# Inverse square roots by one GpSimd power and one Newton step, and an instruction order searched anew

## The chip, the cores and the metric

The kernel runs on one core of a Trainium2 chip. The metric is the time of one execution in device microseconds (us); the profiler's span, from the first to the last instruction of the program, is a little shorter. The engines are called TensorE (PE in the rows; PEld is its weight load), VectorE (DVE), ScalarE (ACT), GpSimd (POOL) and SyncE (SP, which issues the loads).

## What is computed

Two blocks of a network for 512 positions and a width of 1024, all in float32. The first block normalises its input, projects it once, and runs two branches side by side: a recurrence over the positions (a state of 64 x 64 for each of 8 heads) and an attention over the 128 best keys of each query. The second block has two convolutions, an attention to a memory of 256 rows, three gates and a gated feed-forward layer. What matters here is that inverse square roots stand between the stages:

```python
def rmsnorm(x, g):
    xf = x.astype(jnp.float32)
    y = xf * lax.rsqrt(jnp.mean(xf * xf, axis=-1, keepdims=True) + NORM_EPS)
    return (y * g.astype(jnp.float32)).astype(x.dtype)
...
    kk = kk / jnp.maximum(jnp.sqrt(jnp.sum(kk * kk, axis=-1, keepdims=True)), 1e-12)
...
    y = rwkv7_scan(r, decay, k, v, kk, a)
    mu = jnp.mean(y, axis=-1, keepdims=True)
    var = jnp.mean(jnp.square(y - mu), axis=-1, keepdims=True)
    y = (y - mu) * lax.rsqrt(var + GN_EPS) * gn_g.astype(f32) + gn_b.astype(f32)
...
    _, idx = lax.top_k(score, topk)
```

## The kernel before

Activations lie with the width on the 128 partitions and the 512 positions along the free axis, in 76 buffers of 128x512 (`a`). A weight tile of 1024 rows by 128 columns (`wr`, 128x1024 in SBUF, four buffers) is loaded by SyncE, rounded by ScalarE into `wh`, and the rest is put into `wl` by VectorE (line 354). TensorE then forms a product of 128x512 out of 24 matmuls (eight times `wh` by the rounded activation, `wh` by its rest, `wl` by the rounded activation) in one of eight PSUM buffers (`ps`). Nearly every instruction passes through one helper, so its line is 341; lines 345 to 361 are helpers that may choose between two engines.

The work before the second block is called the **first part** here. It has these strands:

- the projections of the first block (24 weight tiles: k, r, v, latent, gates);
- the decay, the pair matrices of eight chunks of 64 positions, their inverse (31 dependent pairs of a product and an addition on VectorE, then small matmuls), and the **chain**: eight chunks, each needing the state of the one before;
- a group norm after each second chunk (four, `gn0` to `gn3`);
- the index scores, and for three blocks of queries sixteen rounds of a maximum of eight and a replacement on VectorE (`topk1` to `topk3`, tiles of 256, 384 and 512 columns);
- the attention heads (`att0` to `att3`);
- the memory: its norm, its keys (`memk0` to `memk7`: eight float32 products of 128x256 each, 16 records in the trace), and its values in two halves (`memv0`, `memv1`: 48 matmuls of 128x512 each; here the weights are the moving side, so the rows read `ps<-wh,a` and `ps<-wl,a`);
- the splits `y0` to `y7` of the two branches' results into a rounded half and a rest, on which the first matmuls of the output projection (`out0` to `out7`, first half; then the second half and all of the second block) wait.

The second block follows: long rows of dense matmuls, with 31-tap convolutions on VectorE beside them.

The order on every engine is made ahead of time by a planner in the file (class `Program`). It gives every operation a duration from a cost table, keeps a clock for each engine, and always takes the operation that can start first; where several can, the one of lowest rank. A rank is an operation's place in the source plus a level of its group, from the table `LEVEL`. So a change of the table moves operations on all engines, and the engines then run their lists strictly in order.

An inverse root, `rsqrt`, is called 15 times: nine times in the first part (the input's norm, the key norm of the recurrence, the index keys, the index queries, the memory, four group norms), twice between the blocks, once in the convolution's layer norm, once before the feed-forward layer, and once for each half of the output. Each call works on a tile `s` of 2 to 32 columns: one tensor_scalar that scales and adds epsilon, two integer instructions for a first guess, and three Newton steps of three instructions each, all on VectorE, each depending on the one before.

Of the kernel before, what the change touches and what calls it, by code (L numbers as in the profile page):

```python
# [8 lines left out]
F32 = mybir.dt.float32  # L9
F32R = mybir.dt.float32r  # L10
AF = mybir.ActivationFunctionType
ALU = mybir.AluOpType
# [13 lines left out]
NA = 76  # L26
NS = 12
LEVEL = {
# [12 lines left out]
}  # L41
MEMC = 4
BOOST = 0
# [43 lines left out]
class Program:  # L87
# [73 lines left out]
    def cost(self, who, op, outs, ins):  # L161
        n = outs[0].free_size()
# [9 lines left out]
        n = max(x.free_size() for x in outs + ins)  # L172
# [10 lines left out]
            return 0.069 + 0.064 * (scalar or narrow > 0 and op == "tensor_scalar") + n / (1920.0 if fast else 960.0)  # L183
        if who == "S":
            return (0.058 if ins[0].space == PSUM else 0.085) + 0.092 * (narrow + len(outs) - 1) + n / 1175.0
        return 0.07 + n / (1250.0 if op == "memset" else 440.0)

    def order(self):
        nodes = self.nodes
# [129 lines left out]
def build(tc, I, O, plan=None):  # L319
# [69 lines left out]
    def here():  # L389
        return len(prog.nodes) - 1  # L390

    V, S, G, PE, SY = (Queue(e, w) for e, w in ((nc.vector, "V"), (nc.scalar, "S"), (nc.gpsimd, "G"),
                                                 (nc.tensor, "PE"), (nc.sync, "SY")))
# [13 lines left out]
    cst = es.enter_context(tc.tile_pool(name="cst", bufs=1))  # L407
# [42 lines left out]
    for k in range(8):  # L450
        t = A()
# [30 lines left out]
    G.memset(hsum, 0.0)  # L482
    G.memset(hsum[0:64, 0:1], 1.0)
    G.memset(hsum[64:128, 1:2], 1.0)
    hav = cst.tile([128, 1], F32, name="hav")
    G.memset(hav, 1.0 / 64)
    chmask = A((128, 8, 64))
# [25 lines left out]
    def ts(eng, out, in0, s1, s2, op0, op1=None):  # L513
        if op1 is None:
            eng.tensor_scalar(out, in0, s1, None, op0=op0)
        else:
            eng.tensor_scalar(out, in0, s1, s2, op0=op0, op1=op1)
# [8 lines left out]
    ts(G, DP("hbg", 24), P_("b_gate", 0, 24), 0.5, None, ALU.mult)  # L526
    ts(G, DP("hln", 16), P_("ln_g", 0, 16), 0.5, None, ALU.mult)

    I32 = mybir.dt.int32

    def rsqrt(src, n, eps, op=ALU.add, scale=1.0):

        x, y, t = SM(n), SM(n), SM(n)
        ts(V, x, src, scale, eps, ALU.mult, op)
        ts(V, t.bitcast(I32), x.bitcast(I32), 1, None, ALU.logical_shift_right)
        ts(V, y.bitcast(I32), t.bitcast(I32), -1.0, float(0x5F3759DF), ALU.mult, ALU.add)
        for _ in range(3):
            V.tensor_mul(t, y, y)
            V.scalar_tensor_tensor(t, t, -0.5, x, op0=ALU.mult, op1=ALU.mult)
            V.scalar_tensor_tensor(y, t, 1.5, y, op0=ALU.add, op1=ALU.mult)  # L540
        return y


# [155 lines left out]
    for j in range(2):  # L699
        t = A()  # L700
# [638 lines left out]
    r2 = SM(4)  # L1339
# [358 lines left out]
```

## Time and profile before

| | us |
|---|---|
| median of three runs (1376.52 to 1382.12) | 1377.17 |
| the profiled execution: its time | 1377.95 |
| the profiled execution: its span | 1376.2 |
| TensorE busy | 1348.1 |
| VectorE busy | 1049.8 |
| ScalarE busy | 585.4 |
| GpSimd busy | 29.9 |

Busy time is the union of an engine's instructions. A matmul counts as busy while it waits in the pipeline, so a busy TensorE may still do little useful work; how dense it is can be read from how fast one matmul of 128x512 starts after another.

### The profile page before, as it was taken

The numbers are of one execution on the slowest core, as the hardware profiler recorded it, in microseconds if no ns is written. First come the engines' busy times: TensorE is split into PE (matmuls) and PEld (weight loads), VectorE is DVE, ScalarE is ACT, GpSimd is POOL, SyncE is SP. The second block draws the span as 40 slices with busy tenths as digits, with TensorE's granted clock in tenths as the row PEclk, the third lists the DMA queues.
The fourth block names the chain that finished last, engine by engine and source line by source line (L and its number), as shares of the span: only waits on it lengthen the run. The fifth ranks groups of instructions, "written<-read, shape, count | busy, mean of one in ns | idle before, by whom it ended". The sixth has DMA issues, their size and how long they took to land.

```text
span 1376.2 us, 18233 instructions
## 1 busy us (share of the span) xinstructions
PE 1348.1 (98%) x7032; PEld 1121.8 (82%) x7032; DVE 1049.8 (76%) x1902; ACT 585.4 (43%) x945; POOL 29.9 (2%) x68
## 2 busy tenths in 40 slices
PE   7999999999999999999999999999999999999997
PEld 6878877888888888888888878888888888888886
DVE  7699879999699999999993584444577788784333
ACT  6683455668353334322222372223444444442221
POOL 2010002100000000000000000000000000000000
PEclk9999988999999999999999999999999999999999
DMA  6203220031446221233333223233222333322321
GB/s 225 71 20 104 84 72 32 32 100 55 145 146 214 92 77 62 77 101 99 92 98 101 77 92 107 92 98 101 92 92 95 104 92 96 103 88 96 100 70 61
DMA packets 41927, 129.29 MB, mean 94 GB/s; under 512 B 4912, under 2 KB 7088, under 8 KB 41840
## 3 DMA queue, kind: packets, MB, share of 16 engines
q1 hardware_dynamic: 41840, 128.13, 28.8%
q8 instruction: 55, 0.90, 0.3%
q14 instruction: 32, 0.26, 0.1%
HBM read 123.91 MB, written 4.19 MB: 93 GB/s over the span
## 4 chain that ended last, share of the span: by engine, by line
PE 88%; DVE 7%; ACT 3%; issue 1%; POOL 0%; DMA 0%; DVEq 0%; POOLq 0%; ACTq 0%
PE ps L341 88%; DVE a L341 5%; ACT a L341 2%; DVE s L341 1%; DVE wl L354 0%; DVE a L354 0%; ACT a L346 0%; ACT wh L341 0%; DMA wr<-in_w_v 0%; POOL a L341 0%; DVE a L345 0%; POOL mm L341 0%; DVE x L345 0%; ACT a L350 0%; POOL gsel L341 0%
## 5 line engine op out<-in xcount | busy, mean ns | idle before, releaser
L341 PE MATMUL ps<-a,wh 128*128 128x512 f32 (+1 forms) x3276 | 1006.2, 388 | 0.2 <-ACT wh L341 0.2
L341 PEld LDWEIGHTS ps<-a,wh 128*128 128x128 f32 x3276 | 612.1, 188 | 123.5 <-ACT wh L341 0.8
L341 PE MATMUL ps<-a,wl 128*128 128x512 f32 (+1 forms) x1638 | 634.7, 388 | 0.5 <-DVE wl L354 0.5
L341 ACT ACTIVATE wh<-wr 128x1024 fp32r<-128x1024 f32 (+3 forms) x223 | 224.8, 1010 | 490.6 <-PE ps L341 362.3
L341 PEld LDWEIGHTS ps<-a,wl 128*128 128x128 f32 x1638 | 308.2, 188 | 62.8 <-DVE wl L354 1.0
L354 DVE TENSOR_TENSOR wl<-wr,wh 128x1024 fp32r<-128x1024 f32 (+3 forms) x223 | 257.9, 1159 | 78.2 <-ACT wh L341 76.8
L341 DVE SCALAR_TENSOR_TENSOR a<-a,par 128x511 f32<-128x511 f32 (+24 forms) x393 | 273.4, 730 | 5.5 <-ACT a L341 3.1
L341 DVE TENSOR_TENSOR a<-ps,a 128x512 f32<-128x512 f32 (+1 forms) x186 | 117.2, 632 | 113.2 <-PE ps L341 107.2
L341 ACT ACTIVATE a<-a 128x512 f32<-128x512 f32 (+5 forms) x184 | 112.3, 623 | 169.5 <-DVE a L341 151.2
L341 PE MATMUL ps<-a 128*64 128x64 f32 (+10 forms) x1060 | 134.3, 296 | 14.5 <-POOL a L341 7.5
L341 PEld LDWEIGHTS ps<-a 128*64 128x64 f32 (+5 forms) x1040 | 103.5, 170 | 27.3 <-DVE a L341 5.7
L341 DVE SCALAR_TENSOR_TENSOR a<-a 128x512 f32<-128x512 f32 (+3 forms) x112 | 67.7, 611 | 20.3 <-ACT a L341 19.4
L341 DVE TENSOR_TENSOR a<-a 128x512 f32<-128x512 f32 (+5 forms) x134 | 76.0, 585 | 3.0 <-ACT a L341 1.9
L341 ACT ACTIVATE a<-a,par 128x512 f32<-128x512 f32 (+1 forms) x89 | 65.1, 737 | 19.7 <-DVE a L341 18.0
L354 DVE TENSOR_TENSOR a<-a 128x512 fp32r<-128x512 f32 x72 | 48.4, 686 | 18.1 <-ACT a L341 16.1
L341 ACT ACTIVATE a<-ps 128x512 fp32r<-128x512 f32 (+5 forms) x77 | 42.1, 569 | 44.4 <-PE ps L341 33.5
L341 DVE SCALAR_TENSOR_TENSOR a<-a,ps 128x512 f32<-128x512 f32 x24 | 16.5, 686 | 55.5 <-PE ps L341 55.4
L341 ACT ACTIVATE a<-a,dpar 128x512 f32<-128x512 f32 (+2 forms) x57 | 41.6, 733 | 7.6 <-DVE a L341 7.3
L346 ACT ACTIVATE a<-ps 64x256 f32<-64x256 f32 (+5 forms) x74 | 29.5, 409 | 28.3 <-PE ps L341 26.9
L341 PE MATMUL ps<-ident,a 128*128 128x128 f32 x204 | 32.7, 286 | 1.0 <-ACT a L350 0.6
L341 PEld LDWEIGHTS ps<-ident,a 128*128 128x128 f32 x204 | 25.8, 155 | 7.2 <-ACT a L350 1.7
L341 PE MATMUL ps<-a,wr 128*128 128x256 f32 x128 | 29.6, 379 | 0.0
(113 smaller groups left out, 567.7 us busy)
## 6 DMA issues: line engine op xcount, KB each, us to landing
wr<-in_w_in SPq DMA_DIRECT2D x96, 512.0 KB, 3.6
wr<-in_w_up SPq DMA_DIRECT2D x44, 512.0 KB, 3.4
wr<-in_w_down SPq DMA_DIRECT2D x16, 512.0 KB, 3.5
a<-in_xt SPq DMA_DIRECT2D x16, 256.0 KB, 3.5
wr<-in_w_k SPq DMA_DIRECT2D x8, 512.0 KB, 3.6
wr<-in_w_v SPq DMA_DIRECT2D x8, 512.0 KB, 3.6
wr<-in_w_out SPq DMA_DIRECT2D x16, 256.0 KB, 2.7
wr<-in_w_att SPq DMA_DIRECT2D x8, 512.0 KB, 3.5
```

Source lines behind the costliest of these rows:

```text
L341: prog.add({self.who: (op, lambda: f(*a, **k))}, outs, ins)
L346: "S": ("activation", lambda: nc.scalar.activation(out, src, AF.Copy))}, [out], [src])
L354: prog.add({"V": ("tensor_sub", lambda: nc.vector.tensor_sub(out, x, y))}, [out], [x, y])
```

## The change

`rsqrt` keeps its first instruction, takes the power -0.5 of the result on GpSimd (a tensor_tensor against a constant tile `mhalf` of 128x32, filled once at the start), and makes one Newton step on VectorE. That is four VectorE instructions for twelve, and a handover to GpSimd and back. The planner's cost of a tensor_tensor on GpSimd rises by 0.5 us (the products of the chain are called tensor_mul there and keep theirs), and all 76 levels have new values.

```diff
 LEVEL = {
-    "att0": -0.214, "att1": 1.055, "att2": -0.113, "att3": 1.636, "base": 2.048, "chain": -0.643, "first":
+    "att0": -0.233, "att1": 0.828, "att2": 3.274, "att3": -0.202, "base": -0.147, "chain": -0.334, "first":
...
-    "memk4": 1.634, "memk5": 1.165, "memk6": -1.209, "memk7": 3.877, "memv0": -0.227, "memv1": -0.052, "norm":
+    "memk4": 3.276, "memk5": -0.212, "memk6": -1.07, "memk7": 3.939, "memv0": 3.63, "memv1": -0.234, "norm":
...
-        return 0.07 + n / (1250.0 if op == "memset" else 440.0)
+        return 0.07 + 0.5 * (op == "tensor_tensor") + n / (1250.0 if op == "memset" else 440.0)
...
+    mhalf = cst.tile([128, 32], F32, name="mhalf")
+    G.memset(mhalf, -0.5)
...
     def rsqrt(src, n, eps, op=ALU.add, scale=1.0):
 
         x, y, t = SM(n), SM(n), SM(n)
         ts(V, x, src, scale, eps, ALU.mult, op)
-        ts(V, t.bitcast(I32), x.bitcast(I32), 1, None, ALU.logical_shift_right)
-        ts(V, y.bitcast(I32), t.bitcast(I32), -1.0, float(0x5F3759DF), ALU.mult, ALU.add)
-        for _ in range(3):
-            V.tensor_mul(t, y, y)
-            V.scalar_tensor_tensor(t, t, -0.5, x, op0=ALU.mult, op1=ALU.mult)
-            V.scalar_tensor_tensor(y, t, 1.5, y, op0=ALU.add, op1=ALU.mult)
+        G.tensor_tensor(y, x, mhalf[:, 0:n], op=ALU.pow)
+        V.tensor_mul(t, y, y)
+        V.scalar_tensor_tensor(t, t, -0.5, x, op0=ALU.mult, op1=ALU.mult)
+        V.scalar_tensor_tensor(y, t, 1.5, y, op0=ALU.add, op1=ALU.mult)
         return y
```

Three places show what this does to the order. The first is VectorE at the root of the index queries (8 columns); `wr` and `x` with two sizes are the inverse's products and additions. Before:

```order
L341 TENSOR_SCALAR s<-ps 128x8
L341 TENSOR_TENSOR wr<-wr,a 128x23x9
L341 TENSOR_SCALAR s<-s 128x8
L341 TENSOR_TENSOR a<-wr,x_367 128x192
L341 TENSOR_SCALAR s<-s 128x8
L341 TENSOR_TENSOR wr<-wr,a 128x24x8
L341 TENSOR_TENSOR s<-s 128x8
L341 TENSOR_TENSOR a<-wr,x_367 128x175
L341 SCALAR_TENSOR_TENSOR s<-s 128x8
```

After, the same root is complete in:

```order
L341 TENSOR_SCALAR s<-ps 128x8
L341 SCALAR_TENSOR_TENSOR a<-a 128x512 x2
L341 TENSOR_TENSOR s<-s 128x8
L341 TENSOR_TENSOR a<-ps,a 128x512
L341 SCALAR_TENSOR_TENSOR s<-s 128x8
L354 TENSOR_TENSOR wl<-wr,wh 128x1024
L341 SCALAR_TENSOR_TENSOR s<-s 128x8
```

The root no longer stands between the steps of the inverse, and two gate products of 128x512 stand between its first instruction and the one that needs GpSimd's result.

The second is TensorE at the first half of the memory's values, `memv0`. Before, it begins in the middle of the attention:

```order
L341 MATMUL ps<-a 128x384 x2
L341 MATMUL ps<-a,wr 128x256 x8
L341 MATMUL ps<-a 128x128 x2
L341 MATMUL ps<-wh,a 128x512
L341 MATMUL ps<-ident,a 128x128
L341 MATMUL ps<-wl,a 128x512
L341 MATMUL ps<-wh,a 128x512 x2
```

After, it begins where the first half of the output projection (rows `a,wh` and `a,wl`) ends:

```order
L341 MATMUL ps<-a,wl 128x512
L341 MATMUL ps<-a,wh 128x512 x2
L341 MATMUL ps<-a,wl 128x512
L341 MATMUL ps<-wh,a 128x512
L341 MATMUL ps<-wl,a 128x512
L341 MATMUL ps<-wh,a 128x512 x2
```

All 48 matmuls of `memv0` have moved from the first part to behind it; the last memory key, `memk7`, has gone the other way.

The third is VectorE at the memory's norm, of which only the order after is shown (before, the four squares stand on ScalarE, line 360):

```order
L341 MATCH_REPLACE a<-s,a 128x512
L341 SCALAR_TENSOR_TENSOR a<-a,wi 128x384
L341 MAX s<-a 128x8
L361 TENSOR_TENSOR a<-a 128x512 x3
L341 TENSOR_TENSOR a<-a 128x512
```

Three of the four squares of the memory now stand on VectorE.

## Rows read from the trace of the kernel before

**Rows 1.** The page's busy times: engine, busy us (share of span), instructions.

```profile
PE 1348.1 (98%) x7032; PEld 1121.8 (82%) x7032; DVE 1049.8 (76%) x1902; ACT 585.4 (43%) x945; POOL 29.9 (2%) x68
```

**Rows 2.** Busy time by stretch; the columns stand in the first line.

```profile
core 0: us, PE busy (x) PEld busy (x) DVE busy (x) ACT busy (x) POOL busy (x), PEclk, DMA share, GB/s
0.00:65.00 65.00, 57.18 (x281) 46.43 (x282) 46.20 (x91) 42.22 (x69) 8.18 (x36) 1.00 0.48 157
...
140.00:195.00 55.00, 53.88 (x385) 44.88 (x384) 40.15 (x88) 25.77 (x40) 1.90 (x2) 0.94 0.26 82
195.00:275.00 80.00, 73.52 (x818) 63.09 (x818) 75.93 (x237) 49.18 (x117) 11.55 (x21) 0.91 0.11 38
275.00:352.50 77.50, 76.70 (x503) 64.98 (x502) 76.94 (x260) 55.95 (x135) 0.00 (x0) 1.00 0.25 79
352.50:1364.00 1011.50, 1010.75 (x4622) 841.63 (x4623) 731.85 (x1071) 365.50 (x484) 1.44 (x2) 1.00 0.31 99
```

**Rows 3.** TensorE's timeline at the first part's end: start, duration, engine, operation.

```profile
348.78 3.71 PE L341 MATMUL ps<-a 128*64 128x128 f32 x64
352.42 0.73 PE L341 MATMUL ps<-a,wh 128*128 128x512 f32 x2
...
374.34 3.61 PE L341 MATMUL ps<-a,wr 128*128 128x256 f32 x16
```

**Rows 4.** TensorE's timeline inside `memv0`.

```profile
285.54 0.62 PE L341 MATMUL ps<-wh,a 128*128 128x512 f32 x2
285.99 0.39 PE L341 MATMUL ps<-wl,a 128*128 128x512 f32 x1
286.22 0.62 PE L341 MATMUL ps<-wh,a 128*128 128x512 f32 x2
```

**Rows 5.** VectorE's timeline: the splits `y0` to `y2`, then `y3` behind one of `memk5`.

```profile
349.32 1.89 DVE L354 TENSOR_TENSOR a<-a 128x512 fp32r<-128x512 f32 x3
...
351.93 1.29 DVE L354 TENSOR_TENSOR a<-a 128x512 fp32r<-128x512 f32 x2
```

**Rows 6.** Timeline of the last root, which stands alone, and of TensorE behind it.

```profile
1366.04 0.16 DVE L341 TENSOR_SCALAR s<-ps 128x2 f32<-128x2 f32 x1 [1.37 <-PE ps L341]
1366.23 0.37 DVE L341 TENSOR_SCALAR s<-s 128x2 int32<-128x2 int32 x2
...
1368.01 0.36 DVE L341 SCALAR_TENSOR_TENSOR s<-s 128x2 f32<-128x2 f32 x2
...
1368.42 0.71 PE L341 MATMUL ps<-ident,s 128*128 128x128 f32 x4 [1.52 <-DVE s L341]
```

**Rows 7.** VectorE's timeline where the index root stands between the inverse's steps.

```profile
147.34 0.38 DVE L341 TENSOR_TENSOR wr<-wr,a 128x207 f32<-128x207 f32 x1
147.63 0.17 DVE L341 TENSOR_SCALAR s<-s 128x8 int32<-128x8 int32 x1
147.75 0.53 DVE L341 TENSOR_TENSOR a<-wr,x 128x192 f32<-128x192 f32 x1
```

**Rows 8.** VectorE's groups by shape: line, operation, count | busy us, mean ns.

```profile
L354 DVE TENSOR_TENSOR wl<-wr,wh 128x1024 fp32r<-128x1024 f32 x195 | 237.8, 1221 | 70.4 <-ACT wh L341 68.9
...
L341 DVE SCALAR_TENSOR_TENSOR a<-a 128x512 f32<-128x512 f32 x72 | 49.6, 689 | 20.3 <-ACT a L341 19.4
```

**Rows 9.** The one square that VectorE makes: count, duration min/median/max in ns.

```profile
L361 DVE TENSOR_TENSOR a<-a x1: 685/685/685, 13.1 to 13.1; 128x512 f32<-128x512 f32 x1
```

**Rows 10.** GpSimd's groups by shape: count | busy us, mean ns.

```profile
L341 POOL TENSOR_SCALAR_AFFINE_SELECT wr<-wr 128x1024 f32<-128x1024 f32 x1 | 2.9, 2932 | 0.1
...
L341 POOL TENSOR_SCALAR dpar<-par 128x16 f32<-128x16 f32 x1 | 0.7, 737 | 0.0
...
L341 POOL MEMSET hsum<- 128x2 f32 x1 | 0.1, 101 | 0.0
```

**Rows 11.** GpSimd's twelve products in the chain: duration min/median/max in ns, first and last start.

```profile
L341 POOL TENSOR_TENSOR a<-a,pc x12: 616/617/619, 208.0 to 257.0; 128x256 f32<-128x256 f32 x12
```

**Rows 12.** Timeline of a handover from ScalarE to GpSimd.

```profile
1369.63 0.38 ACT L341 ACTIVATE a<-ps 128x256 f32<-128x256 f32 x1 [4.50 <-DVE a L341]
...
1370.09 1.41 POOL L341 TENSOR_TENSOR a<-a 128x256 f32<-128x256 f32 x2 [7.90 <-ACT a L341]
```

More of the change, by code (lines that the diff above doesn't have):

```diff
@@ L527, in build @@
     ts(G, DP("hln", 16), P_("ln_g", 0, 16), 0.5, None, ALU.mult)
-    I32 = mybir.dt.int32
     def rsqrt(src, n, eps, op=ALU.add, scale=1.0):
```

20 rows, old and new, of the table LEVEL are left out of this document.

## The prediction

> **What bounds the kernel now.** I read the page's busy times first. TensorE is busy for 1348.1 of 1376.2 us and VectorE for 1049.8 [rows 1], so at first sight only 28 us could be had. That is a mean over two unlike parts, so I took the busy times by stretch next. From 352.5 to 1364 TensorE is busy for 1010.75 of 1011.5 us, while VectorE has 280 us to spare [rows 2]. Nothing that VectorE saves there can show: this part is the sum of its matmuls, and it stays as long as it is. In the first part it is the other way round. From 195 to 275 us VectorE is busy for 75.93 of 80, and from 275 to 352.5 for 76.94 of 77.5 [rows 2]: 4.6 us of idle time in 157.5. TensorE also looks busy there, but these are matmuls that wait in its pipeline, and its granted clock from 195 to 275 is 0.91, so it spent 0.09 x 80 x 2 = 14 us at the lower of its two levels, 1.2 GHz [rows 2]; it did so in the stretch with the fewest dense matmuls. From 140 to 195 VectorE is idle for 14.85 of 55 us with TensorE busy for 53.9 [rows 2]: there the projections are the limit.
>
> The timelines then show what ends the first part. The last attention matmuls run up to 352.4, and the output projection starts at 352.42 and is dense from there [rows 3]. It needs the splits `y0` to `y3`, which VectorE makes from 349.3 to 353.2 [rows 5]. So the end of the kernel is the time at which VectorE has worked through its list down to these splits, plus all matmuls that are still to be done then, plus a tail of some 10 us. The change can act at these three places only.
>
> **Term 1, VectorE's list ahead of the splits.** Nine of the fifteen roots lie in it, and each loses eight instructions, 72 in all. What one is worth depends on what stands beside it. In a root that stands alone one instruction follows another after (1368.01 - 1366.23) / 9 = 0.2 us [rows 6]; in a full list the next independent instruction begins 0.12 us after a root instruction has begun (147.63 to 147.75) [rows 7]. Where the root's instruction falls between two dependent steps of the inverse, it fills a gap that stays: the product at 147.75 needs the addition that ends at 147.72 [rows 7], so it would not start before that anyway. I take 0.12, because the stretch that counts is full: 72 x 0.12 = 8.6 us. The bounds are half of the 72 at 0.12 (the others in such gaps), 4.3, and all at 0.2, 14.4.
>
> The new order also takes `memv0` out of this list: its four subtractions of 128x1024 at 1.22 us [rows 8] are 4.9 us. In return three squares of the memory come to it from ScalarE, 3 x 0.685 = 2.1 us [rows 9]. Other pieces change places in both directions, and I count them at nothing, with 2 us either way. The list becomes shorter by 8.6 + 4.9 - 2.1 = 11.4 us.
>
> The power is a wait in this list. VectorE runs in order, so everything behind the first Newton instruction waits with it: subtractions of weight rests for TensorE, and the selection. What the wait costs depends on the power's duration, and no power is in the trace. The nearest rows are GpSimd's own: a memset of two columns takes 0.10 us, a tensor_scalar of 16 columns 0.74, the longest instruction (a select over 1024 columns) 2.93 [rows 10], and the chain's products of 256 columns 0.62 [rows 11]. I take 0.74, the row with arithmetic that is nearest in size. A handover to GpSimd took 0.08 us (ScalarE ends at 1370.01, GpSimd starts at 1370.09) [rows 12]; I take the same for the way back. So the answer comes 0.9 us after the question. At the index root two products of 128x512 at 0.69 us [rows 8] stand in between, 1.4 us, and by the order six others have about 1 to 2 us. The wait is hidden at 0.74. It would not be at more than about 1.1, taking 1.2 us as the common cover. The first two roots (input norm and key norm) have next to no cover, but VectorE is idle for 18.8 of the first 65 us [rows 2]. GpSimd has little else to do, 29.9 us in all [rows 1].
>
> The chain's twelve products ran on GpSimd while VectorE was 95% busy, and each took 616 to 619 ns [rows 11], so I see no sign that VectorE's traffic slows GpSimd. On the start of the first power the Trainium skill speaks against the change: by GPSIMD Engine Reference, section 2.1, the first call of a freshly loaded GpSimd kernel pays about 6 us for loading its code. No run here shows that: the first of the twelve products, at 208.0, lies in the same 3 ns as the others [rows 11]. By that figure, if all of it were exposed, the sum would come out at 1378.4 instead of 1372.4.
>
> **Term 2, the matmuls left at the splits.** `memv0` now comes behind the first half of the output projection. Its 48 matmuls follow each other at (286.22 - 285.54) / 3 = 0.227 us [rows 4], together 10.9 us, and they are added to the dense part. The memory key `memk7` leaves it: 16 records in 3.6 us [rows 3]. Net 7.3 us more to do after the splits. In the first part nobody misses them, as VectorE sets the pace. This is why the change is worth less than VectorE saves: work that used to fill TensorE's waits has been put where there are none.
>
> **Term 3, the tail.** The last root stands alone. From its first instruction at 1366.04 to the broadcast on TensorE at 1368.42 it takes 2.38 us [rows 6]. The new one is 0.2 for the first instruction, 0.08 + 0.74 + 0.08 for the power, and three Newton instructions, 0.58: 1.68 us, so 0.7 us less. With a power of 2.93 it would be 1.5 us more, with 0.10 it would be 1.3 less. The five other roots after the first part lie under dense matmuls and cost or give nothing.
>
> **Sum.** -11.4 + 7.3 - 0.7 = -4.8 us. Against the profiled execution (span 1376.2, time 1377.95) that is a span of 1371.4 and a time of 1373.2. The median of the runs is 0.8 below the profiled time, so I set it against the median: 1377.17 - 4.8 = 1372.4. A difference of about 0.5%, 6.9 us, is what a measurement of this kernel can tell from no change; this forecast is inside it.
>
> **Rivals.**
>
> *The new order also closes holes.* Of the 14.85 us in which VectorE is idle from 140 to 195 [rows 2], the selection or the gates might fill a half, since the new order starts the selection of the 256-column block before the end of the inverse. Then 7.4 us more go: 1365.0. Against it: TensorE is busy for 53.9 of these 55 us [rows 2], so VectorE is idle because its inputs are late, and only work whose inputs are ready can fill the time.
>
> *The power is dear (the slower side).* If it takes p, each of the seven roots in the full stretches waits p + 0.16 - 1.2, and the tail gets p - 0.74 longer. At the upper row, 2.93, that is 7 x 1.89 + 2.2 = 15.4 us: 1387.8. The gain of 4.8 is gone at 8p = 4.8 + 7.28 + 0.74, p = 1.6 us, and the result is slower by over 0.5% from 8p = 11.7 + 8.02, p = 2.5 us. For it: a power is more than one arithmetic step. Against it: 2 to 32 columns are little work beside the 256 columns that took 0.62 us [rows 11].
>
> *The chain is left without filling.* By the new order the first four chunks of the chain have no dense matmuls between their small ones. TensorE fell to the lower level in just this stretch before, at a loss of 0.09 x 80 = 7.2 us of full-speed time [rows 2]. If that loss doubles and VectorE, which waits for the chain's results, is held up by all of it, the time is 1372.4 + 7.2 = 1379.6. Against it: the selection has work for VectorE all the while.
>
> *It does less than it says.* If half of the removed instructions lay in gaps between dependent steps, term 1 is 4.3 us smaller: 1376.7, no change at all.
>
> **How the numbers follow.** The forecast, with the last rival in its own spread of 1369 to 1377, gets 0.50; closed holes 0.25; a dear power 0.12; a bare chain 0.13. The predicted time is that of the likeliest, 1372.4. The range leaves out half of the dear powers (those above 2.2 us) and a part of the holes, those that give more than 9 us: 1363 to 1385. Faster by over 0.5% means below 1370.3: most of the closed holes (0.22) and a fifth of the forecast (0.10), 0.32. Slower by over 0.5%, above 1384.1: half of the dear powers (0.06) and the worst of the bare chain (0.03), 0.09. Within: 0.59.
>
> **What the profile of the changed kernel would show.** Right: the output projection starts about 11 us earlier, near 341, VectorE is idle for no more than 5 us in the 150 before, and `memv0` stands in the dense part as 11 us. Each power is about 0.7 us. The broadcast of the last root comes 1.7 us after its first instruction. Wrong: an output projection that starts at 335 or earlier (holes closed), VectorE's idle time ended by GpSimd in several places (a dear power), or more than 14 us at the lower clock level between 195 and 275 (a bare chain). A dense part that is not longer by 7 us would mean that I have placed the moved matmuls wrongly.

## The result and the profile after

The changed kernel takes 1392.5 us (median of 4 runs, 1392.4 to 1394.6) beside 1377.4 for the kernel before: 1.0092 times its time, 95% interval 1.0069 to 1.0116. The forecast was 1372.4, in a range up to 1385. In the profiled executions the span went from 1376.2 to 1390.7, by 14.5 us.

The busy times of the page, the kernel after, answer [rows 1]: VectorE lost 10.0 us of work and GpSimd gained 23.3; TensorE has the same 7032 instructions.

```profile
PE 1350.3 (97%) x7032; PEld 1121.7 (81%) x7032; DVE 1039.8 (75%) x1788; ACT 582.6 (42%) x939; POOL 53.2 (4%) x84
```

Busy times by stretch, after, with the columns of [rows 2]:

```profile
0.00:65.00 65.00, 54.16 (x254) 42.87 (x255) 39.29 (x65) 38.78 (x62) 13.60 (x39) 0.98 0.46 149
195.00:275.00 80.00, 69.41 (x884) 60.60 (x884) 75.35 (x203) 43.63 (x100) 17.25 (x23) 0.91 0.14 44
275.00:352.50 77.50, 73.47 (x519) 61.97 (x518) 70.32 (x241) 52.41 (x137) 4.87 (x3) 1.00 0.16 52
352.50:1364.00 1011.50, 1008.32 (x4547) 835.45 (x4546) 732.24 (x1042) 375.19 (x500) 4.03 (x4) 1.00 0.32 100
```

VectorE is idle for 25.7 us of the first 65 (18.8 before) and for 7.2 ahead of 352.5 (0.6 before), and the dense part now has TensorE idle for 3.2 us. The same view for the whole list up to the end of the rest of `y3`, first before, then after:

```profile
0.00:353.20 353.20, 335.29 (x2393) 278.61 (x2394) 314.04 (x815) 219.08 (x459) 27.08 (x64) 0.97 0.25 80
```

```profile
0.00:358.70 358.70, 330.10 (x2371) 273.45 (x2372) 306.74 (x746) 211.15 (x448) 44.92 (x74) 0.98 0.24 75
```

VectorE's busy time fell by 7.3 us, its idle time rose from 39.2 to 52.0, by 12.8, and the splits are 5.5 us later. TensorE's timeline, after, shows what that does to the output projection [rows 3]; the second and third rows are the first and the last record of `memv0`, and the fourth begins the second half of the projection. Behind it stands the row that begins this half before:

```profile
355.32 1.31 PE L341 MATMUL ps<-a,wh 128*128 128x512 f32 x3
...
377.55 0.39 PE L341 MATMUL ps<-wh,a 128*128 128x512 f32 x1
...
388.21 0.39 PE L341 MATMUL ps<-wh,a 128*128 128x512 f32 x1
388.43 0.62 PE L341 MATMUL ps<-a,wh 128*128 128x512 f32 x2
```

```profile
377.60 0.81 PE L341 MATMUL ps<-a,wh 128*128 128x512 f32 x2
```

The out projection starts 2.9 us later (352.42 before). Its second half starts at 388.4 against 377.6, 10.8 later; from there to the end 3.7 us more are lost.

The powers by shape, after (GpSimd's groups, columns as in [rows 10]), the first two of them in the timeline, and VectorE's wait behind the second:

```profile
L341 POOL TENSOR_TENSOR s<-s,mhalf 128x8 f32<-128x8 f32 x5 | 8.5, 1702 | 93.1 <-DVE s L341 93.1
L341 POOL TENSOR_TENSOR s<-s,mhalf 128x4 f32<-128x4 f32 x6 | 6.1, 1018 | 687.7 <-DVE s L341 687.7
L341 POOL TENSOR_TENSOR s<-s,mhalf 128x32 f32<-128x32 f32 x1 | 5.4, 5432 | 31.5 <-DVE s L341 31.5
L341 POOL TENSOR_TENSOR s<-s,mhalf 128x2 f32<-128x2 f32 x3 | 2.1, 700 | 356.4 <-DVE s L341 356.4
```

```profile
23.61 1.07 POOL L341 TENSOR_TENSOR s<-s,mhalf 128x4 f32<-128x4 f32 x1 [5.19 <-DVE s L341]
56.17 5.43 POOL L341 TENSOR_TENSOR s<-s,mhalf 128x32 f32<-128x32 f32 x1 [31.48 <-DVE s L341]
```

```profile
61.63 0.19 DVE L341 TENSOR_TENSOR s<-s 128x32 f32<-128x32 f32 x1 [5.54 <-POOL s L341]
```

A power takes 0.70 us for 2 columns, 1.02 for 4, 1.70 for 8 and 5.43 for 32. The shortest and the longest give 4.73 / 30 = 0.158 us a column. The planner was told 0.0023 a column, and the prediction took 0.74 for every size. Behind the 32-column power, the root of the key norm, VectorE stands for 5.5 us. In all, VectorE waits for roots from GpSimd 12 times, 16.0 us; six of these waits, 9.6 us, lie ahead of the splits (the list of waits, over the whole span and from 0 to 358.7: total, times, longest):

```profile
DVE s L341 <- POOL s L341: 16.0, 12, 5.5
```

```profile
DVE s L341 <- POOL s L341: 9.6, 6, 5.5
```

### The profile page after: what moved, and what is told of

Same layout as the page of the kernel before. It is cut to its first block, busy times and chain, and to the rows that moved or that the text cites. A ratio compares the mean times of both kernels' runs of the same rounds, so it can differ in the third digit from the quotient of the medians.

```text
span 1390.7 us, 18142 instructions
## 1 busy us (share of the span) xinstructions
PE 1350.3 (97%) x7032; PEld 1121.7 (81%) x7032; DVE 1039.8 (75%) x1788; ACT 582.6 (42%) x939; POOL 53.2 (4%) x84
## 4 chain that ended last, share of the span: by engine, by line
PE 85%; DVE 9%; ACT 3%; POOL 1%; issue 1%; DMA 0%; SPq 0%; DVEq 0%; ACTq 0%; POOLq 0%
PE ps L341 85%; DVE a L341 6%; ACT a L341 2%; DVE s L341 1%; POOL s L341 1%; DVE a L354 1%; DVE wl L354 1%; ACT wh L341 1%; DVE a L345 1%; DMA a<-in_xt 0%; ACT a L360 0%; DVE a L349 0%; DVE x L345 0%; DVE a L361 0%; ACT x L341 0%
## 5 line engine op out<-in xcount | busy, mean ns | idle before, releaser
L341 DVE SCALAR_TENSOR_TENSOR a<-a,par 128x510 f32<-128x510 f32 (+23 forms) x393 | 272.5, 731 | 4.7 <-ACT a L341 2.6
L341 ACT ACTIVATE a<-a 128x512 fp32r<-128x512 f32 (+4 forms) x184 | 112.4, 623 | 168.8 <-DVE a L341 161.7
L341 POOL TENSOR_TENSOR s<-s,mhalf 128x4 f32<-128x4 f32 (+3 forms) x15 | 22.1, 1477 | 1168.7 <-DVE s L341 1168.7
```

What stands on the lines that cost most here:

```text
L341: prog.add({self.who: (op, lambda: f(*a, **k))}, outs, ins)
```

## The experiments

Those with "after" or "changed kernel" in their expectation keep the changed kernel's order, those with "before" the order before, unless a new one is named. Ratios are against the kernel before on the same chip, whose medians lay between 1378 and 1380 us. Differences to the changed kernel's 1392.5 go from chip to chip, beside 1377.4 for the kernel before there, so 1 to 2 us of them tell nothing. The same holds for single profiles: three kernels with one and the same list up to the out projection (after, e5, e7) start it at 355.32, 356.39 and 356.15.

### The power's price, and the order's

**The 32-column root alone back on VectorE**, at its place in the new order.

```diff
-        G.tensor_tensor(y, x, mhalf[:, 0:n], op=ALU.pow)
+        prog.add({"G": ("tensor_tensor", guess if n == 32 else power)}, [y], [x, mhalf[:, 0:n]])
```

(`guess` issues the guess and two Newton steps on VectorE where the power stood.)

> The changed kernel with its own order on every engine; only the key norm's root (32 columns) has its power replaced, at the same place, by the old guess and two Newton steps on VectorE. Theory A (the power of 32 columns, 5.43 us in the trace, holds up VectorE and then TensorE, which waits for the root's broadcast): the root takes about 2.4 us for 6.1, so 3.8 us less, 1388.7 us. Theory B (the new order loses the time, the powers lie beside other work): within 1 us of 1392.5.

Measured: 1388.3 us, ratio 1.0068 (1.0052 to 1.0083), 4.2 us less than the changed kernel (3.3 by the ratios, whose intervals overlap): theory A, which the trace bears out. The root's last Newton step now begins at 57.53 us instead of the 61.63 above, and the out projection starts at 349.87, 5.4 us earlier, of which 4.2 are left at the end of the span:

```profile
57.53 0.19 DVE L341 TENSOR_TENSOR s<-s 128x32 f32<-128x32 f32 x1
```

**All fifteen back on VectorE**, in the new order (`guess if True`).

> The new order with the old roots: all fifteen powers are replaced at their places by the guess and two Newton steps on VectorE. Theory A: against e1 the other powers' waits in the first part go (0.94 + 0.64 + 0.39 + 1.16 = 3.1 us in the trace) and 64 instructions at 0.12 us come (7.7), so about 1393. Theory B: within 2 us of 1392.5 as well. What it tells by itself is the order's share: its time less that of the kernel before is what the new order does with the old roots.

Measured: 1399.5 us, ratio 1.0149 (1.0134 to 1.0164). Both theories missed. With old roots the new order is 21 us slower than the order before, and 11 us slower than with only the long one old: the short powers do earn something in an order made for short roots (the eight old steps stand in one lump here, without the instructions between them that the order before has). TensorE's list has the roots' broadcasts early there, and waits for them 11.2 us (in the kernel after 4.4):

```profile
PE ps L341 <- DVE s L341: 11.2, 10, 3.3
```

**The order before with the powers**: all of them, and all but the 32-column one.

```diff
-        ts(V, y.bitcast(I32), t.bitcast(I32), -1.0, float(0x5F3759DF), ALU.mult, ALU.add)
+                nc.gpsimd.tensor_tensor(y, x, mhalf[:, 0:n], op=ALU.pow)
```

(with the shift and two of the three Newton steps left out, the tile of -0.5 filled at the start, and nothing else moved)

> The order of the kernel before, with the new root at each of the fifteen places (power on GpSimd where the second integer instruction stood, the last Newton step kept, the first two left out). Theory A: the key norm's root costs 3.8 us more, the other roots of the first part free about 6.7 us of VectorE and wait for about 6, so 1380 to 1381. Theory B: the powers are no burden and VectorE's list gets shorter by 8.6 us: 1368 to 1370.

> As the one before, but the key norm's root (32 columns) stays on VectorE. Theory A: 3.8 us less than that, about 1376.8, the same as the kernel before. Theory B: the same as the one before within 1 us, 1368 to 1370.

Measured: 1382.4 (1.0029, 1.0016 to 1.0042) and 1380.5 (1.0003, 0.9991 to 1.0015). Theory A both times: in the order before the powers give nothing, and the long one costs 2 to 4 us (1.9 by the medians, 3.6 by the ratios).

### The dense part

**Two instructions of two neighbouring weight blocks moved ahead.** In the kernel after TensorE waits once for 3 us in the dense part, for a block that ScalarE rounds behind 16 scalings of other tiles. The timelines of ScalarE, VectorE and TensorE, after:

```profile
822.96 1.04 ACT L341 ACTIVATE wh<-wr 128x1024 fp32r<-128x1024 f32 x1
```

```profile
822.74 1.22 DVE L354 TENSOR_TENSOR wl<-wr,wh 128x1024 fp32r<-128x1024 f32 x1
```

```profile
824.05 0.79 PE L341 MATMUL ps<-a,wh 128*128 128x512 f32 x1 [3.00 <-ACT wh L341]
```

```diff
         seq = prog.order()
+        for node, behind in ((5962, 5768), (5934, 5773)):
+            seq.remove(node)
+            seq.insert(seq.index(behind) + 1, node)
```

> The changed kernel in its own order, with two instructions moved in the dense part: ScalarE's rounding of one weight block (wh, 128x1024, at 822.96 in the changed kernel's trace) goes ahead of 12 scalings, and VectorE's rest of the block before it (wl, at 822.74) ahead of 8 others. Theory A: the dense part's 3.0 us wait of TensorE for this block is a real loss that came with the new order, and everything behind it moves up: 1392.5 - 3.0 = 1389.5 us, and the longest wait of TensorE for wh is gone. Rival B: the matmuls behind it wait for something else that is late by the same amount (the residual sums on VectorE, now pushed back by 1.2 us): 1392.5, within 1.

Measured: 1388.6 us, ratio 1.0065 (1.0047 to 1.0083), 3.9 less than the changed kernel: theory A. From 800 to 1000 us TensorE is busy for 199.89 of 200 where it was busy for 196.92. The wait was not the whole loss. Behind these 3.0 us without a matmul, TensorE's granted clock in the kernel after is 0.57 from 824 to 828 us, so most of this stretch ran at the lower of its two levels, 1.2 GHz:

```profile
824.00:828.00 4.00, 3.95 (x10) 3.15 (x11) 4.00 (x6) 4.00 (x7) 0.00 (x0) 0.57 0.56 155
```

That is another (1 - 0.57) x 4 = 1.7 us of full-speed time. In e1, whose 3.01 us of wait are the same, the clock from 818.5 to 826.5 is 0.61, where the kernel after has 0.79 over the like 8 us: 1.4 us more lost, and so 5.4 us at the out projection became 4.2 at the end.

**Both together.**

> The changed kernel in its own order, with the two edits of e1_kk_newton and e5_weights_early together: the 32-column root by guess and Newton steps on VectorE, and the two weight instructions of the dense part moved ahead. Theory A: the two losses lie one behind the other and add up: 1392.5 - 4.2 - 3.9 = 1384.4 us; what is then left against the kernel before is the 7 us of the matmuls moved to the dense part. Rival B: the weight wait was only there because the first part was late, or is back with another timing: 1388.3, as with e1 alone.

Measured: 1382.8 us, ratio 1.0017 (0.9999 to 1.0035), span 1382.4. Theory A: the two losses add up, 8.3 of the 14.5 us of span. What is left, 6.2, is about the 7.3 of the moved matmuls.

**46 of the 48 matmuls of `memv0` left out**, in the new order and in the order before.

```diff
-                            PE.matmul(ps[kb], mH[kk][:, c], H[:, k, :], start=kk == 0, stop=False)
+                            (PE if kk == 0 else NO).matmul(ps[kb], mH[kk][:, c], H[:, k, :], start=kk == 0, stop=half == 0)
```

(and `NO` for the other two matmuls of the first half; `NO` issues nothing)

> The changed kernel in its own order; of the 48 matmuls of the memory values memv0 46 are left out, so these values are not the reference's; loads, roundings, copies and splits stay. Theory A (term 2): they stand where TensorE sets the pace, and all of them count: 46 x 0.227 = 10.4 us less, 1382.1 us. Rival B: the dense part waits for its weights' rounding and rests on ScalarE and VectorE there, and gets back half of it or less: above 1387.

> The kernel before in its own order, with the same 46 matmuls of memv0 left out, which stand ahead of the output projection there. Theory A (term 2): VectorE sets the pace there, and the matmuls fill TensorE's waits: 0 to 3 us less than before, 1375 to 1378. Rival B: TensorE set the pace in this stretch as well, so that moving the matmuls behind it was no loss: 10.4 us less, 1367.

Measured: after 1392.5 (1.0088, 1.0056 to 1.0119), nothing gained; before 1381.3 (1.0001, 0.9987 to 1.0015), nothing gained either. The second is theory A, the first is not: the matmuls behind `memv0` start 7.7 us earlier (380.70, 388.43 above) and then wait for their weights, with the clock lower behind the waits (0.90 from 378 to 395, 0.92 from 395 to 410). TensorE's timeline, new order without `memv0`:

```profile
380.70 0.73 PE L341 MATMUL ps<-a,wh 128*128 128x512 f32 x2 [1.94 <-ACT wh L341]
384.02 0.79 PE L341 MATMUL ps<-a,wl 128*128 128x512 f32 x1 [2.59 <-DVE wl L354]
...
406.99 0.50 PE L341 MATMUL ps<-a,wl 128*128 128x512 f32 x1 [1.87 <-DVE wl L354]
```

**Its loads left out too** (three of its four weight blocks, with rounding and rests).

> The changed kernel in its own order, with 46 of the 48 matmuls of the memory values memv0 left out as in e7_after_no_memv0, and now also the loads, roundings and rests of three of their four weight blocks, so these values are not the reference's. In e7 the matmuls behind the gap began up to 9.8 us earlier and had lost all of it by 410-420 us, with TensorE waiting for wh (1.94) and wl (2.59, 1.87). Theory A: what took the gain back there was the supply of rounded weights, three of whose blocks were memv0's own; without them the whole of 10.4 us shows: 1392.5 - 10.4 = 1382.1 us. Rival B: behind the first half of the out projection TensorE must wait for something else until about 415 us (the first residual sums and their norm, or the loads behind), and memv0 fills this wait: 1392.5, within 1.5, so that the move of memv0 cost nothing by itself.

Measured: 1388.0 us, ratio 1.0071 (1.0052 to 1.0091), which overlaps the changed kernel's; 4.5 us less by the medians, 5.9 by the spans, of which 1.2 lie ahead of the out projection (354.13). Between the two theories: about half of the 10.4 us arrives. The rest goes into a load that comes late and into rests of weights on VectorE, which is busy for all of the 15 us from 395 to 410 (ScalarE and TensorE, this kernel):

```profile
374.94 0.63 ACT L341 ACTIVATE wh<-wr 128x512 fp32r<-128x512 f32 x1 [3.36 <-DMA wr<-in_w_out]
```

```profile
379.21 0.50 PE L341 MATMUL ps<-a,wl 128*128 128x512 f32 x1 [1.72 <-DVE wl L354]
...
401.30 0.50 PE L341 MATMUL ps<-a,wl 128*128 128x512 f32 x1 [1.88 <-DVE wl L354]
```

So moved matmuls are paid for in the sum of the dense part, but at this place they also cover waits that would be there without them. What the move cost by itself is not shown: nothing by e7, about half of the 10.4 us by e9.

### The first part

**Two memory keys left out.** In the new order 30 records of `memk2` and `memk0` stand on TensorE ahead of the attention, and VectorE waits (TensorE and VectorE, after):

```profile
315.85 6.64 PE L341 MATMUL ps<-a,wr 128*128 128x256 f32 x30
```

```profile
323.20 0.69 DVE L345 COPY a<-ps 128x512 f32<-128x512 f32 x1 [4.09 <-PE ps L341]
```

```diff
-                    PE.matmul(ps[:, :256], w[:, k, :], rows(k), start=k == 0, stop=k == 7)
+                    (NO if n in (0, 2) and k else PE).matmul(ps[:, :256], w[:, k, :], rows(k), start=k == 0, stop=k == 7 or n in (0, 2))
```

> The changed kernel in its own order; of the memory keys memk0 and memk2 only the first of eight matmuls each is left, so these keys are not the reference's; loads, copies and splits stay. It takes 14 matmuls of two passes (about 6 us of TensorE) from just ahead of the attention, where VectorE waited 4.09 us for TensorE. Theory A: TensorE's list, with these matmuls ahead of the attention, is where a part of VectorE's saving went, and the splits come earlier by the 4 us that VectorE waited: 1392.5 - 4 = 1388.5 us. Theory B: VectorE waits for the attention's inputs anyway, or gets the time back only to wait later: 1392.5, within 1. The whole 6 us would mean that TensorE alone sets the pace there: 1386.5.

Measured: 1390.2 us, ratio 1.0069 (1.0044 to 1.0094), which overlaps the changed kernel's. In the profile the out projection starts at 351.99, 3.3 us earlier, and the span is 3.7 shorter. That is nearer to theory A; the timed runs alone don't settle it.

**Short roots without any power.** A guess in one instruction and one Newton step, all on VectorE: the lower bound for any cheaper root. First in the order before.

```diff
-        ts(V, t.bitcast(I32), x.bitcast(I32), 1, None, ALU.logical_shift_right)
-        ts(V, y.bitcast(I32), t.bitcast(I32), -1.0, float(0x5F3759DF), ALU.mult, ALU.add)
-        for _ in range(3):
+        nc.vector.tensor_scalar(y.bitcast(I32), x.bitcast(I32), -0.5, float(0x5F3759DF), op0=ALU.mult, op1=ALU.add)
```

> The kernel before in its own order; each root keeps its first instruction, a guess in one instruction instead of two, and one Newton step instead of three, all on VectorE, with no power: 7 of 11 instructions are gone and no wait is added (the roots are exact to some tenths of a per cent only). It is the most that any cheaper root could give in this order. Theory A: VectorE's full list is not what sets the end of the first part; it is full because it works while TensorE and VectorE pass the inverse, the chain and the attention to each other, and the saving comes back as waits: 0 to 3 us less than before, of it 1.4 in the tail (7 instructions of 0.2 us, which stand alone there). Rival B (term 1 of the prediction): VectorE's list sets it: 9 roots x 7 x 0.12 = 7.6 us, and 1.4 in the tail: 9.0 us less.

Measured: 1378.6 us, ratio 0.9987 (0.9970 to 1.0005). Theory A. VectorE has 5.0 us less to do up to 353.2, and the out projection starts 0.2 us earlier than in [rows 3] (VectorE's stretch, then TensorE's timeline, this kernel):

```profile
0.00:353.20 353.20, 334.55 (x2394) 277.65 (x2395) 309.08 (x752) 218.92 (x459) 26.26 (x64) 0.98 0.25 80
```

```profile
352.24 0.73 PE L341 MATMUL ps<-a,wh 128*128 128x512 f32 x2
```

**The same in the new order**, each at its power's place.

> The changed kernel in its own order; each power is replaced by a guess in one instruction on VectorE at its place, so that no root waits for GpSimd (the roots are exact to some tenths of a per cent only, since one Newton step is all that is left). Theory A: of the power's 16.0 us of waits on VectorE only the 5.5 at the 32-column root and the 0.9 in the tail reach the end: 1392.5 - 5.5 - 0.7 = 1386.3 us, some 2 us below e1_key_root_and_weights' neighbour e1_kk_newton (1388.3), and still slower than before. Rival B: the waits of the other roots (0.64, 0.94, 0.39, 1.16) add up on the path as well, and the new order with a free root is as fast as the prediction had it: 1392.5 - 16 = 1376.5 us.

Measured: 1380.3 us, ratio 1.0011 (0.9997 to 1.0024), span 1378.3, 12.4 less than the changed kernel's. Between the theories, nearer to B. Aligned from the back, the two traces part by 0.6 us in the tail, 2.7 in the dense part and 9.1 up to the out projection (TensorE's timeline, then VectorE's list up to the splits, this kernel):

```profile
346.25 1.31 PE L341 MATMUL ps<-a,wh 128*128 128x512 f32 x3
```

```profile
0.00:349.60 349.60, 329.18 (x2371) 273.36 (x2372) 307.12 (x755) 210.87 (x448) 30.06 (x65) 0.98 0.25 77
```

Of the 2.7 some 1.5 lie behind the weight block's wait, which is here too (3.01 us): this time the clock stays at 1.00 behind it (814.1 to 818.1). That is not the powers' doing, so they are worth about 11 of the 12.4 us. And with short roots this order has a list 6.9 us shorter than the order before (307.12, 314.04) and starts the out projection 6.2 us earlier.

**Short roots and no `memv0`, in the order before.**

> The kernel before in its own order, with the edits of e11_before_short_roots and e8_before_no_memv0 together: short roots (exact to some tenths of a per cent) and 46 of memv0's 48 matmuls left out, so these values are not the reference's. Alone the first moved nothing ahead of the out projection and the second nothing at all. Theory A: VectorE and TensorE are both full in the 77.5 us ahead of the out projection (76.94 and 76.70 busy), and each takes back what is taken from the other; together they give what VectorE's list has lost in the full stretches, 33 root instructions that had 2.9 us there by the traces: 2 to 3 us ahead of the out projection and 1.5 in the tail, 3.5 to 4.5 us less than before, at least 2 less than e11. Rival B: a chain of dependent steps through both engines sets the pace, and neither list does: as e11, 1.5 us less than before, within 1.

Measured: 1376.7 us, ratio 0.9979 (0.9965 to 0.9993). By the ratio it is 0.8 thousandths below the short roots alone, with intervals that overlap. This does not tell the two theories apart, though A's 2 us less than e11 are not seen beyond that. Its profile does not tell either: there the granted clock is 0.95 from 65 to 140 us, 1.00 in e11's, and the out projection starts 2.5 us later, at 354.78. Why both lists look full in the order before stays open.

### Is it the power, or the order?

**A planner that knows the price.** The 32-column root stays on VectorE with three Newton steps; the power's price becomes the measured one (only the powers are called tensor_tensor on GpSimd, so the products of the chain keep theirs, other than the expectation says); the levels are searched anew.

```diff
-        return 0.07 + 0.5 * (op == "tensor_tensor") + n / (1250.0 if op == "memset" else 440.0)
+        return 0.38 + n / 6.3 if op == "tensor_tensor" else 0.07 + n / (1250.0 if op == "memset" else 440.0)
```

> The changed kernel with a new order by the same planner: it is told the measured price of GpSimd's products and powers (0.38 us + 0.158 per column, where the changed kernel's planner has 0.57 + 0.0023 per column), the 32-column root goes back to a guess and three Newton steps on VectorE, and the levels were searched anew for the planned end. Theory A: the changed kernel lost by its power's price being unknown to its planner; by its own plan this one ends 4.9 us ahead of the changed kernel's, and with the weight wait (3.9) and the key root (4.2) gone it is at 1380 or below, as fast as the kernel before or faster by up to 5 us. Rival B: the power's latency costs more than a plan sees (VectorE's queue waits in order behind each), and it stays above 1382.

Measured: 1373.95 us, ratio 0.9959 (0.9944 to 0.9973); the time is theory A's. Price, long root and levels were changed together, so the share of each is not shown. Again, on another chip:

> The kernel of e14_power_price_order again, with more runs, beside the same runs of the kernel before. Theory A: the gain stands: ratio 0.996, 5 to 6 us below the kernel before, and the interval excludes 1. Rival B: it was within what runs of one kernel differ by: ratio 0.998 to 1.001.

Measured: 1373.9 us, ratio 0.9957 (0.9940 to 0.9974). It beats both kernels. `memv0` stands behind the first splits here too, but the out projection starts 12.9 us earlier than before in e14's profile (340.87 and so 11.6 earlier in e17's), and VectorE waits 6.1 us for powers instead of 16.0 (TensorE's timeline, stretches, list of waits, e14):

```profile
339.55 0.74 PE L328 MATMUL ps<-a,wh 128*128 128x512 f32 x2
```

```profile
195.00:275.00 80.00, 69.25 (x929) 60.28 (x928) 78.06 (x226) 46.09 (x108) 14.60 (x22) 0.96 0.14 45
275.00:352.50 77.50, 76.10 (x504) 64.88 (x503) 72.98 (x241) 51.58 (x130) 5.12 (x3) 1.00 0.25 76
```

```profile
DVE s L328 <- POOL s L328: 6.1, 6, 1.2
```

**The same order without its powers** (eight instructions on VectorE at each power's place).

> The order of e14_power_price_order, unchanged; the powers of 2, 4 and 8 columns are replaced, each at its place, by the guess and two Newton steps of the kernel before on VectorE (the third step stays where it is). Theory A: the gain of e14 needs the power: eight dependent instructions of about 0.2 us stand where the power's 0.7 to 1.6 us and its handover stood, and VectorE cannot do anything else meanwhile: 7 us or more above e14, at least as slow as the kernel before, 1380 or above (in the changed kernel's order the same exchange cost 11 us, e1 against e2). Rival B: the gain is the search's, and the root does not matter in that order: 1374 to 1376, as e14.

Measured: 1391.5 us, ratio 1.0076 (1.0052 to 1.0100), 17.6 us above that order with its powers: theory A. The out projection starts at 353.81. The eight steps stand there in one lump, so this is the price of long roots in that order, not the best they could have.

**Short roots with an order of their own**: guess and two Newton steps with fitted constants on VectorE, levels searched anew.

```diff
+        ts(V, y.bitcast(I32), x.bitcast(I32), -0.5, float(0x5F376908), ALU.mult, ALU.add)
+        for c in (1.5008789, 1.5000006):
```

> No power at all: each root is a guess in one instruction and two Newton steps with constants fitted to them (error below 1e-6), 7 instructions on VectorE instead of 11, and the order is searched anew with that by the same planner. Theory A: what the roots can give lies in their latency on VectorE, without a handover to GpSimd; by its plan it ends 1.8 us ahead of the kernel before's, so 1372 to 1379 on the chip. Rival B: a new order by these plans loses some 5 us on the chip against the kernel before's, whatever the root, since plan and chip differ by that: 1380 to 1386.

Measured: 1379.0 us, ratio 0.9992 (0.9981 to 1.0003): theory A's mechanism gave no gain that can be told from none; the time is at A's upper end. So the order with powers is 5 us ahead of this one. How long each search ran is not on record, and there is one order of each kind: how much of the 5 us is the searches' luck stays open.

## Why the prediction was wrong

**Two steps failed.** The larger is the wait for the powers, which the prediction put at nothing ("The wait is hidden at 0.74"). VectorE waited 9.6 us for six of them ahead of the splits, and with short roots in the same order the out projection starts 9.1 us earlier (e12). The sign that the prediction gave for a dear power, VectorE's idle time ended by GpSimd in several places, is there, and VectorE is idle for 11.8 us from 195 to 352.5, not for 5 or less.

**The power's price was mis-sized**, and with it the cover. I took 0.74 for every size from a row of 16 columns of another operation [rows 10] and held 2 to 32 columns for little work beside 256 columns of a product [rows 11]. It is 0.70 at 2 columns, but 1.02 at 4, 1.70 at 8 and 5.43 at 32. I let the key norm's root go free because VectorE is idle for 18.8 us of the first 65. Those idle times lie elsewhere; at this root VectorE's own next products and rests queue behind it, and everything to the end moves with it: 4.2 us (e1). The rival "the power is dear" had the right mechanism. Its break-even, 1.6 us, is passed at 8 columns, but it used one price for seven roots and left out the one that costs most. The five later roots, which were to cost nothing, cost about 1.2 us more than short ones (e12, without the 1.5 of the clock).

**The other step** is the one from term 1 to the sum: that the splits come earlier by what VectorE's list is shorter. The list is 7.3 us shorter, not 11.4. By the time that each instruction adds to the list, the narrow root instructions lost 7.7 (forecast 8.6), the weight rests 5.0 (4.9), the squares added 2.1 (2.1), and the pieces counted at nothing about 3. In the order before, 5.0 us less on VectorE moved the out projection by 0.2 (e11). [rows 2] showed VectorE full for 157 us, and I read full as limiting. TensorE was busy for 76.70 of the last 77.5 us beside it, which I explained away; the runs don't settle whether that list or a chain through both engines holds the end there, only that VectorE's list alone does not. In the new order with short roots, 6.9 us less came out as 6.2 (e12), but there TensorE's list is shorter as well, by the moved matmuls, so this is no test of the step.

**Term 2** had the right sum: the second half of the out projection starts 10.8 us later, of it 2.9 from the first part and 7.9 beside a forecast of 7.3. A part of the difference is a reading: `memk7` occupies TensorE for 3.3 us, from 374.34 to the next start at 377.60, and not for the 3.6 of its record, so the net is 7.6. That these matmuls were free where they stood is borne out (e8). That they cost their full time behind the splits is true of the sum only: without them the weights are late (e7, e9).

**The dense part** was to stay as long as it was but for term 2. A new order may also put an engine's list wrong there: a weight block rounded behind 16 scalings cost 3.9 us (e5). No step of the prediction looked for that.

**Term 3** came out right, with some luck: the 0.74 of another operation on 16 columns happens to fit a power of 2 columns. The last root's four steps, after, answer [rows 6]:

```profile
1381.30 0.16 DVE L341 TENSOR_SCALAR s<-ps 128x2 f32<-128x2 f32 x1 [1.37 <-PE ps L341]
1381.54 0.70 POOL L341 TENSOR_TENSOR s<-s,mhalf 128x2 f32<-128x2 f32 x1 [4.83 <-DVE s L341]
1382.27 0.16 DVE L341 TENSOR_TENSOR s<-s 128x2 f32<-128x2 f32 x1 [0.81 <-POOL s L341]
...
1382.88 0.71 PE L341 MATMUL ps<-ident,s 128*128 128x128 f32 x4 [0.72 <-DVE s L341]
```

From 1381.30 to 1382.88 are 1.58 us, with 1.68 forecast and 2.38 before.

**VectorE's traffic.** The prediction saw no sign that it slows GpSimd, from twelve equal products [rows 11]. The trace after has such signs (GpSimd, then VectorE at the same time):

```profile
253.06 3.02 POOL L341 TENSOR_SCALAR_AFFINE_SELECT a<-a 128x128 f32<-128x128 f32 x1 [3.38 <-DVE a L341]
257.19 1.05 POOL L341 TENSOR_TENSOR a<-a,pc 128x256 f32<-128x256 f32 x1 [1.12 <-DVE a L341]
```

```profile
253.45 1.87 DVE L361 TENSOR_TENSOR a<-a 128x512 f32<-128x512 f32 x3
257.08 0.69 DVE L341 TENSOR_TENSOR a<-a 128x512 f32<-128x512 f32 x1
```

The select takes 0.29 us at two other places of this trace, and most of the chain's products still take 0.62; the slow select lies beside the three squares that the change moved to VectorE. Both rows are as long in e1 (3.02 and 1.05). The first power of 8 columns, beside two products of 128x512, took 1.96 us, the second 1.64. That VectorE's instructions beside them are the cause is argued from this, not isolated, and what it cost is not shown.

**The other rivals.** The chain was not barer in its clock: 0.91 from 195 to 275, as before. No holes closed: from 140 to 195 VectorE is idle for 12.9 us, 14.9 before. The first power took 1.07 us, the five others of its size 1.01 on average, and it began 0.09 us after its input was ready, so the 6 us for loading code, which the Trainium skill gives in GPSIMD Engine Reference, section 2.1, do not show here.

**The account** of the 14.5 us of span: key root 4.2 and weight block 3.8, by e1 and e5 and together 8.3 by e10; the moved matmuls 7.3 by the sum of both lists, which no run shows by itself; the remainder, about -1, is what the rest of the change gave, the other powers' waits set against the shorter list. Against the forecast the span is 19.3 us too long: about 10.3 by the powers' waits (e12: 9.1 ahead of the out projection, 1.2 behind it), 3.8 by the weight block (e5), and 5.2 because even with short roots the out projection starts at 346.25 and not near 341. Each of these is good to about 1 us. What holds back the last 5.2 stays open; by its size it could be what VectorE's list saved less than forecast (6.9 for 11.4 in e12).

## What to carry to other kernels

An engine that is full is not thereby the one that sets the end: take work from it in the old order, as a bound, before pricing a saving by its list. A planner is only as good as its prices: the power lost 0.9% in an order made with a guessed price, and gained 0.4% in one made with the measured price, where the one size that does not pay was left out as well. After a new search, look at the stretch that was to stay as it was for a single late instruction.

## What the hardware showed that was not expected

GpSimd's power is slow by the column: 0.70, 1.02, 1.70 and 5.43 us for 2, 4, 8 and 32 columns of 128 partitions, some 0.158 us a column, where a product of 256 columns on the same engine takes 0.616 to 0.619 us [rows 11]. Beside full-size instructions of VectorE, one of GpSimd's took ten times as long as elsewhere (a select of 128x128 3.02 us for 0.29) and a product 1.05 for 0.62. A stop of 3.0 us in TensorE's dense part was followed by the lower clock in the kernel after (0.57 over 4 us) and by none in e12 (1.00), so one and the same wait cost 1.7 us more in one profile than in another. And 7 of 11 root instructions less in a row of VectorE that looks full moved TensorE by 0.2 us, while the same cut was worth 19 us in an order where the steps of a root stand in one lump (e2 against e12).
